# The samples' memory attention of a streaming encoder step: split float32r products against native fp32 products in 32-column tiles

## The chip, the cores and the metric

The kernel runs on one core of one Trainium2 chip. Such a core has five engines with their own instruction streams: TensorE multiplies matrices (the profile shows its products as PE and its weight loads as PEld), VectorE (DVE) and ScalarE (ACT) work on rows of data and can read TensorE's results in PSUM, GpSimd (POOL) works on SBUF, and SyncE (SP) issues most of the DMAs. The metric is the device time of one execution in microseconds (us); less is better. Data are float32 throughout. A product in plain float32 and one in "float32r" are two forms of the same TensorE instruction; the kernel reaches float32 accuracy with float32r by splitting an operand into a rounded part and the rest ("hi" and "lo"), and adding the products of the parts.

## The reference, cut to what matters

One layer of an encoder works on a prompt of 2048 frames and on 8 running streams ("samples") with 16 new frames each, 128 rows in all. After the mixer each group does cross-attention with 4 heads of 256 channels into 256 memory tokens. For the prompt the keys and values are computed; every sample brings its own cached ones (`cache_mem_k`, `cache_mem_v`, 8 x 256 x 4 x 256 each).

```python
def memory_attention(h, mk, mv, w_mq, w_mo):
    B, T, _ = h.shape
    q = (h @ w_mq).reshape(B, T, MEM_HEADS, MEM_HEAD_DIM)
    s = jnp.einsum("bthd,bmhd->bhtm", q, mk, preferred_element_type=jnp.float32) * (MEM_HEAD_DIM ** -0.5)
    p = jax.nn.softmax(s, axis=-1)
    o = jnp.einsum("bhtm,bmhd->bthd", p.astype(mv.dtype), mv).reshape(B, T, D_MODEL)
    return o @ w_mo
```

For the samples this means: each sample multiplies its 16 query rows of 4 heads with its own keys, takes a softmax over 256 tokens per head, and multiplies with its own values.

## The kernel before, in words

The kernel goes through the layer in stages: the prompt's memory keys and values, the input projection with the convolution, band attention, the output projection (`mixout`), cross-attention of the prompt (`phase_cross`) joined with the feed-forward network's first half, and its second half (`down`). The program is recorded by Python code; a scheduler with a timeline model then fixes the order of the instructions on each engine, and puts in the waits. That order is fixed before the run.

The change lies in `mixout` and in the generator `cross_sample` that it drives. `mixout` handles 17 tiles of 128 rows (the samples' tile first, then 16 of the prompt). For each it loads attention and convolution results (`prep`, line 974), splits them, multiplies them with the eight resident blocks of the output weights (`mm3h`, line 298: 48 products of 128x512 per tile, three split products for two halves of eight blocks), and normalises the result into `x1` (lines 1029 to 1035). When the samples' tile is done, `cross_sample` starts. It is a Python generator with a `yield` after each small step; `mixout` lets it take one step after every second block of weights, from the third tile on, so that its work stands between the main products.

The steps of `cross_sample`: normalise the samples' rows; transpose them (`transposed`, lines 1066 to 1078, eight 128x128 transposes, then split); multiply with `w_mq` (`dense`, line 1080); scale and transpose the queries; for each of 16 jobs (sample s, half) load one 128x1024 block of keys (line 1063), split it (`split`, line 1054: ScalarE copies the hi part at line 1057, VectorE subtracts at line 1058), and multiply; softmax; transpose the probabilities; 16 jobs with the values in the same way; transpose the result, multiply with `w_mo`, normalise into `x2`. `Ahead` keeps two jobs loaded (and split) in front of the one being multiplied. Loads go into three buffers ("wf") of 128x1024.

How one job is multiplied before the change: a sample's query block has only 16 columns. GpSimd keeps two zeroed 128x8x128 blocks (`pads`) and copies the 16 columns of the sample's hi part to its own place and those of its lo part to the place 64 columns further (`pad`, lines 1099 to 1104; `blank`, line 1095, clears them again). With that block as weights, one product gives the hi and the lo result in different rows, and the other samples' rows get zeros added. Each job then has eight products of 128x256 in float32r:

```python
for k in range(4):
    kk = 4 * half + k
    for y, r in enumerate((kh, kl)):
        nc.tensor.matmul(sc[:, kk // 2, :], cur[:, kk, :], r[:, k * NM:(k + 1) * NM], ...)
```

After four samples `gather` (line 1110) adds the two halves of the rows into `z`. The jobs with the values (line 1185) look the same. The PSUM tile "so" (4 KB per partition, one buffer) holds in turn the result of `w_mq`, the scores of four samples, the outputs of four samples, and the result of `w_mo`; tile "p" (three buffers) takes transposes.

Other lines that the profile names: L776 and L794 are products in plain float32 of the samples' band attention, L847 transposes there; L937 transposes the sums of the band attention's softmax (128x16); L982 spreads them (16x128); L1225 splits weights for the next stage; L325 to L327 transpose and split the first tiles of the next stage.

Of the kernel before, what the change touches and what calls it, by code (L numbers as in the profile page):

```python
# [140 lines left out]
class Build:  # L141
# [773 lines left out]
    def selectors(self):  # L915

        nc = self.nc
        pool = self.wp = Region().lay(self.fa, 27.5, ("eye", 0.03125, 1), ("rc", 0.03125, 2)).lay(
# [37 lines left out]
    def mixout(self, ctx):  # L956
        nc, A = self.nc, self.A
        sbF, sbR = self.sbF, self.sbR
        fr, ff = self.flex(ctx, (4096, F32R)), self.fa
        pool = (Region().lay(sbF, 34.5, ("wf", 4, 3), ("gbc", 4, 1))  # L960
                .at("ct", 2, (ff, [2, 10])).lay(ff, 0, ("an", 2, 1)).lay(ff, 5, ("po", 4, 1))
                .lay(ff, 12, ("junk", 2, 1), ("xt", 4, 2), ("sh", 4, 1), ("ss", 0.03125, 6), ("rstd", 0.03125, 6),
                     ("nmx", 0.03125, 1), ("sm", 0.03125, 1), ("ri", 0.03125, 1)).lay(ff, 28, ("sgain", 4, 1))
                .lay(fr, 0, ("pad0", 4, 1), ("pad1", 4, 1))
                .at("mh", 4, (sbR, [40, 88])).at("ml", 4, (sbR, [44, 92]))
                .lay(sbR, 96, ("sTh", 4, 1), ("sTl", 4, 1))
                .at("kvh", 4, (sbR, [64, 80]), (fr, [8])).at("kvl", 4, (sbR, [104, 84]), (fr, [12])))
# [73 lines left out]
    def cross_sample(self, pool, ps_so, ps_p):  # L1041
# [24 lines left out]
        def transposed(src, dst, scale=1.0):  # L1066
            th = self.t(pool, [P, KC, P], F32R, "sTh", 1)
            tl = self.t(pool, [P, KC, P], F32R, "sTl", 1)
            for half in range(2):
                sl = slice(4 * half, 4 * half + 4)  # L1070
                pt = self.t(ps_p, [P, 4, P], F32, "p")
                for k in range(4):
                    nc.tensor.transpose(pt[:, k, :], src(4 * half + k), self.ident[:, :])
                nc.scalar.activation(th[:, sl, :], pt[:, :, :], AF.Copy, scale=scale)
                nc.vector.scalar_tensor_tensor(tl[:, sl, :], pt[:, :, :], scale, th[:, sl, :].bitcast(F32),
                                               ALU.mult, ALU.subtract)
                yield
            dst += [th, tl]

# [8 lines left out]
        def places(s):  # L1088


            own = s * DEC_S
            other = (own + 64) % P
            return [slice(o, o + DEC_S) for o in (own, other)]

        def blank(s):
            for c in places(s):
                nc.gpsimd.memset(pads[s % 2][:, :, c].bitcast(F32), 0.0)

        def pad(s, T):
            if s >= 2:  # L1100
                blank(s - 2)
            for c, src in zip(places(s), T):
                nc.gpsimd.tensor_copy(pads[s % 2][:, :, c], src[:, :, s * DEC_S:(s + 1) * DEC_S])
            return pads[s % 2]

        def clear():
            for s in (DEC_B - 2, DEC_B - 1):
                blank(s)

        def gather(dst, src, g):  # L1110

            own, other = slice(g * 64, g * 64 + 64), slice(64 - g * 64, P - g * 64)
            nc.scalar.copy(dst[own], src[other])
            nc.vector.tensor_tensor(dst[own], dst[own], src[own], ALU.add)

        col = lambda x: lambda k: x[:, k * P:(k + 1) * P]
        flat = lambda x: x[:, :, :].rearrange("p a b -> p (a b)")

        hT = []
        yield from transposed(col(h), hT)  # L1120
# [5 lines left out]
        qT = []  # L1126
        yield from transposed(col(q), qT)

        z = self.t(pool, [P, MH, NM], F32, "sh", 1)
        jobs = [(s, b) for s in range(DEC_B) for b in range(2)]  # L1130

        def keys(s, half):
            return split(load(A["cache_mem_kT"][s, half])[:, :])

        ahead = Ahead([lambda j=j: keys(*j) for j in jobs])
        pd = pad(0, qT)
        yield
        for x, (s, half) in enumerate(jobs):
            kh, kl = next(ahead)
            cur = pd  # L1140
            if half == 1 and s + 1 < DEC_B:
                pd = pad(s + 1, qT)
            if half == 0 and s % 4 == 0:
                sc = self.t(ps_so, [P, MH, NM], F32, "so")
            for k in range(4):
                kk = 4 * half + k
                for y, r in enumerate((kh, kl)):
                    nc.tensor.matmul(sc[:, kk // 2, :], cur[:, kk, :], r[:, k * NM:(k + 1) * NM],
                                     start=s % 4 == 0 and kk % 4 == 0 and y == 0,
                                     stop=s % 4 == 3 and kk % 4 == 3 and y == 1, skip_group_check=True)  # L1150
            if half == 1 and s % 4 == 3:
                gather(z, sc, s // 4)
            yield
        clear()
        nmx = self.t(pool, [P, MH], F32, "nmx", 1)
        nc.vector.tensor_reduce(nmx[:, :], z[:, :, :], axis=AX.X, op=ALU.max, negate=True)
        sm = self.t(pool, [P, MH], F32, "sm", 1)
# [17 lines left out]
        for x, (s, b) in enumerate(jobs):  # L1175
            vh, vl = next(ahead)
            cur = pd
            if b == 1 and s + 1 < DEC_B:
                pd = pad(s + 1, pT)
# [519 lines left out]
```

## Time and profile before

| | |
|---|---|
| time, median of 3 runs | 2955.26 us (2954.59 to 2962.31) |
| profiled execution, its own time | 2962.86 us |
| its span | 2960.8 us |
| mean granted TensorE clock | 0.995 |
| TensorE products busy | 2905.3 us (98%) |
| VectorE / ScalarE / GpSimd busy | 2131.0 / 1338.0 / 1418.2 us |
| stage `mixout` with `cross_sample` | about 873 to 1150 us of the span |

A row of the profile that describes a group reads: line, engine, operation, output<-inputs by tile names, shape, count | busy time in us, mean ns of one | idle time of the engine before them and what ended it. Rows of the order of time begin with start and length in us; a count at the end merges equal neighbours, and square brackets give the idle time in front. Product records on TensorE overlap, since a product's record includes the time until its result has left the array; the pace is the distance of starts, not the length of a record. Rows by stretches give, for each engine, busy time and count, then the granted clock, the share of the DMA engines, and GB/s.

### The profile page before, as it was taken

The numbers are of one execution on the slowest core, as the hardware profiler recorded it, in microseconds if no ns is written. First come the engines' busy times: TensorE is split into PE (matmuls) and PEld (weight loads), VectorE is DVE, ScalarE is ACT, GpSimd is POOL, SyncE is SP. The second block draws the span as 40 slices with busy tenths as digits, with TensorE's granted clock in tenths as the row PEclk, the third lists the DMA queues.
The fourth block names the chain that finished last, engine by engine and source line by source line (L and its number), as shares of the span: only waits on it lengthen the run. The fifth ranks groups of instructions, "written<-read, shape, count | busy, mean of one in ns | idle before, by whom it ended". The sixth has DMA issues, their size and how long they took to land.

```text
span 2960.8 us, 45532 instructions
## 1 busy us (share of the span) xinstructions
PE 2905.3 (98%) x16680; PEld 2670.8 (90%) x16680; DVE 2131.0 (72%) x3074; ACT 1338.0 (45%) x2631; POOL 1418.2 (48%) x1334
## 2 busy tenths in 40 slices
PE   9999999989999999999999999999999999999998
PEld 8999999989987887887879999999999999888787
DVE  6787895888875666344459888787888998546666
ACT  4435465678883445233334333433344444333433
POOL 1358496731113344144457555465656775424413
PEclk9999999999999999999999999999999999999999
DMA  8735253665535656133355333544334446756664
GB/s 287 243 129 187 95 166 112 220 212 174 200 125 177 212 201 200 57 114 109 123 173 193 135 123 128 194 163 149 141 132 158 149 142 212 236 169 213 224 224 147
DMA packets 201458, 499.53 MB, mean 169 GB/s; under 512 B 19801, under 2 KB 91361, under 8 KB 192394
## 3 DMA queue, kind: packets, MB, share of 16 engines
q1 hardware_dynamic: 186306, 427.01, 43.6%
q0 software_dynamic: 14928, 69.61, 6.3%
q8 instruction: 131, 2.15, 0.3%
q14 instruction: 93, 0.76, 0.1%
HBM read 365.45 MB, written 141.81 MB: 171 GB/s over the span
## 4 chain that ended last, share of the span: by engine, by line
PE 40%; DVE 3%; DMA 3%; POOL 3%; issue 2%; ACT 1%; SPq 0%; DVEq 0%; POOLq 0%; ACTq 0%
PE psb L292 13%; PE psb L290 13%; PE psb L291 13%; DMA sbf<-in_w_down_dram 1%; PE psb L298 1%; POOL sbf L1512 1%; DMA sbf<-x 1%; DVE sbr L1582 1%; PE psb L1367 1%; DVE sbr L1390 0%; POOL sbf L348 0%; DVE sbx L1390 0%; DMA sbf<-hn 0%; DVE sbf L365 0%; DMA hn<-sbf 0%
## 5 line engine op out<-in xcount | busy, mean ns | idle before, releaser
L290 PE MATMUL psb<-sbr 128*128 128x384 f32 (+3 forms) x2808 | 941.3, 336 | 6.0 <-DVE sbx L657 2.1
L291 PE MATMUL psb<-sbr 128*128 128x384 f32 (+3 forms) x2356 | 804.4, 342 | 0.3
L292 PE MATMUL psb<-sbr 128*128 128x512 f32 (+3 forms) x1848 | 633.4, 344 | 4.6 <-DVE sbr L1582 4.4
L290 PEld LDWEIGHTS psb<-sbr 128*128 128x128 f32 x2808 | 530.3, 189 | 36.6 <-ACT sbr L1581 4.0
L292 PE MATMUL psb<-sbr,sbx 128*128 128x384 f32 (+2 forms) x1484 | 476.2, 322 | 0.0
L291 PEld LDWEIGHTS psb<-sbr 128*128 128x128 f32 x2356 | 444.9, 189 | 27.0 <-DVE sbr L340 0.9
L292 PEld LDWEIGHTS psb<-sbr 128*128 128x128 f32 x1848 | 347.9, 189 | 36.2 <-DVE sbr L1582 9.5
L298 PE MATMUL psb<-sbr 128*128 128x512 f32 x1200 | 295.0, 396 | 5.2 <-DVE flexb L1033 2.8
L1390 DVE TENSOR_TENSOR sbr<-sbf,sbr 128x512 fp32r<-128x512 f32 x258 | 264.4, 1028 | 40.5 <-ACT sbr L1389 39.6
L1389 ACT CAST sbr<-sbf 128x512 fp32r<-128x512 f32 x258 | 159.2, 620 | 278.8 <-PE psb L291 229.1
L292 PEld LDWEIGHTS psb<-sbr,sbx 128*128 128x128 f32 x1484 | 280.6, 189 | 0.1
L298 PEld LDWEIGHTS psb<-sbr 128*128 128x128 f32 x1200 | 223.6, 190 | 52.9 <-DVE flexb L1033 3.2
L523 DVE SCALAR_TENSOR_TENSOR psb<-sbf,psb 128x768 f32<-128x768 f32 (+1 forms) x290 | 264.3, 911 | 6.2
L1582 DVE TENSOR_TENSOR sbr<-sbf,sbr 128x384 fp32r<-128x384 f32 (+2 forms) x242 | 166.0, 710 | 97.5 <-ACT sbr L1581 93.8
L285 POOL TENSOR_TENSOR sbx<-sbf,sbr 128x1024 fp32r<-128x1024 f32 (+1 forms) x62 | 154.4, 2493 | 77.9 <-ACT sbr L283 63.4
L1512 POOL TENSOR_TENSOR sbf<-sbf 128x512 f32<-128x512 f32 x77 | 108.5, 1413 | 168.5 <-DMA sbf<-in_w_down_dram 166.9
L1581 ACT CAST sbr<-sbf 128x384 fp32r<-128x384 f32 (+2 forms) x242 | 112.3, 483 | 168.6 <-PE psb L291 144.1
L533 POOL TENSOR_TENSOR flexb<-flexb,flexb 128x128 f32<-128x128 f32 (+1 forms) x180 | 168.5, 936 | 26.5 <-ACT flexb L532 17.9
L290 PE MATMUL psb<-sbr,sbx 128*128 128x384 f32 (+1 forms) x524 | 170.6, 327 | 0.7 <-ACT sbr L1369 0.7
L1389 ACT CAST sbx<-sbf 128x512 fp32r<-128x512 f32 x153 | 94.7, 620 | 161.4 <-PE psb L291 150.0
L1390 DVE TENSOR_TENSOR sbx<-sbf,sbx 128x512 fp32r<-128x512 f32 x153 | 154.0, 1008 | 14.9 <-ACT sbx L1389 14.6
L1384 POOL TENSOR_TENSOR sbf<-sbf 128x512 f32<-128x512 f32 x66 | 98.3, 1489 | 108.1 <-DVE sbr L1390 50.8
(327 smaller groups left out, 6129.6 us busy)
## 6 DMA issues: line engine op xcount, KB each, us to landing
af<-flexb SPq DMA_DIRECT2D x33, 1344.0 KB, 6.2
sbf<-in_w_down_dram SPq DMA_DIRECT2D x154, 256.0 KB, 3.7
sbf<-in_w_gate_dram SPq DMA_DIRECT2D x66, 512.0 KB, 3.4
sbf<-in_w_up_dram SPq DMA_DIRECT2D x66, 512.0 KB, 3.4
sbf<-af SPq DMA_DIRECT2D x85, 384.0 KB, 4.3
sbf<-x SPq DMA_DIRECT2D x49, 512.0 KB, 3.8
sbf<-in_w_in_dram SPq DMA_DIRECT2D x48, 512.0 KB, 3.9
sbr<-ks POOLq DMA_DIRECT2D x16, 1024.0 KB, 9.1
```

The lines of the kernel that those rows point to most:

```text
L285: self.lo_engine.tensor_tensor(lo[:, c], wf[:, c], hi[:, c].bitcast(F32), ALU.subtract)
L290: nc.tensor.matmul(ps, lh, rh, start=start, stop=False, **kw)
L291: nc.tensor.matmul(ps, lh, rl, start=False, stop=False, **kw)
L292: nc.tensor.matmul(ps, ll, rh, start=False, stop=stop, **kw)
L298: nc.tensor.matmul(y[o], l, r[:, o * 512:(o + 1) * 512], start=start and x == 0, stop=stop and x == 2)
L523: nc.vector.scalar_tensor_tensor(acc if w < CW - 1 else o, src(w), cwt[:, j, w:w + 1], acc, ALU.mult, ALU.add)
L533: nc.gpsimd.tensor_tensor(o, o, v, ALU.add)
L1389: nc.scalar.copy(hs[j][:, :], src[j])
L1390: nc.vector.tensor_tensor(ls[j][:, :], src[j], hs[j][:, :].bitcast(F32), ALU.subtract)
L1512: nc.gpsimd.tensor_tensor(acc[:, :], acc[:, :], q[:, :], ALU.add if s > 0 else ALU.subtract)
L1581: nc.scalar.copy(ch[:, m], a[:, x, m])
L1582: nc.vector.tensor_tensor(cl[:, m], a[:, x, m], ch[:, m].bitcast(F32), ALU.subtract)
```

## The change

The keys and values of the samples are no longer split, and the queries no longer copied into padded blocks. A job now has four products in plain float32, one per head. Each takes 32 columns as weights (16 of the sample and 16 that only fill up: the next sample's queries, or unused rows of the probabilities) and is placed with `tile_position=(0, 32 * head)`, so that head h uses columns 32h to 32h+31 of the array and writes partitions 32h to 32h+31 of PSUM. Scores lie as (head, token) by sample. The host lays out the keys' cache so that one block holds one half of the channels of all four heads.

What follows from that: softmax runs per group of four samples, straight from PSUM (one reduction, four exponentials, a reciprocal, and four scalings, the latter on GpSimd instead of VectorE). Probabilities and outputs have sixteen 128x128 blocks to transpose instead of eight. Queries and probabilities are kept whole (`sT`), without a split. The output is copied out of PSUM after every second sample and split after its transposes, in sixteen small pieces (`token`). The `gather` steps, the blanks and the padded copies go. Splits of `w_mq` and `w_mo` stay. In SBUF some tiles move to make room for the larger `sh` and `sT`, among them the small ones of `selectors`.

```diff
-        fr, ff = self.flex(ctx, (4096, F32R)), self.fa
+        (ft, fr), ff = self.flex(ctx, (2048, F32), (2048, F32R)), self.fa
...
-        pads = [self.t(pool, [P, KC, P], F32R, f"pad{i}", 1) for i in range(2)]
-        for pd in pads:
-            nc.gpsimd.memset(pd[:, :, :].bitcast(F32), 0.0)
-            yield
+        yield
+        yield
+
+        def turn(src, k0):
+            pt = self.t(ps_p, [P, 4, P], F32, "p")
+            for k in range(4):
+                nc.tensor.transpose(pt[:, k, :], src(k0 + k), self.ident[:, :])
+            return pt
+
+        def turned(src, place):
+            th, tl = [self.t(pool, [P, KC, P], F32R, x, 1) for x in ("sTh", "sTl")]
+            for k0 in range(0, len(place), 4):
+                pt = turn(src, k0)
+                some = [p for p in place[k0:k0 + 4] if p]
+                for to, of in some:
+                    nc.scalar.copy(to(th), of(pt))
+                for to, of in some:
+                    nc.vector.tensor_tensor(to(tl), of(pt), to(th).bitcast(F32), ALU.subtract)
+                yield
+            return th, tl
...
+        def heads(out, s, x, left, right):
+            for h_ in range(MH):
+                nc.tensor.matmul(out[32 * h_:32 * h_ + 32, s % 4, :], left(h_), right[:, h_ * NM:(h_ + 1) * NM],
+                                 start=s % 2 == 0 and x == 0, stop=x == 1, tile_position=(0, 32 * h_),
+                                 skip_group_check=True)
...
-        def keys(s, half):
-            return split(load(A["cache_mem_kT"][s, half])[:, :])
...
+        qT = self.t(pool, [P, KC, P + DEC_S], F32, "sT", 1)
+        nc.gpsimd.memset(qT[:, :, P:], 0.0)
+        for k0 in range(0, KC, 4):
+            nc.scalar.copy(qT[:, k0:k0 + 4, :P], turn(col(q), k0)[:, :, :])
+            yield
+        z = self.t(pool, [P, DEC_B, NM], F32, "sh", 1)
+        nmx, sm, ri = [self.t(pool, [P, DEC_B], F32, x, 1) for x in ("nmx", "sm", "ri")]
+        ahead = Ahead([lambda s=s, x=x: load(A["cache_mem_kT"][s, x]) for s, x in jobs])
         yield
+        for s, x in jobs:
+            kx = next(ahead)
+            if x == 0 and s % 4 == 0:
+                sc = self.t(ps_so, [P, 4, NM], F32, "so")
+            heads(sc, s, x, lambda h_: qT[:, 2 * h_ + x, s * DEC_S:(s + 2) * DEC_S], kx)
             yield
+            if x == 1 and s % 4 == 3:
+                g = slice(s - 3, s + 1)
+                nc.vector.tensor_reduce(nmx[:, g], sc[:, :, :], axis=AX.X, op=ALU.max, negate=True)
+                for v in range(s - 3, s + 1):
+                    nc.scalar.activation(z[:, v, :], sc[:, v % 4, :], AF.Exp, bias=nmx[:, v:v + 1],
+                                         accum_out=sm[:, v:v + 1])
+                nc.vector.reciprocal(ri[:, g], sm[:, g])
+                for v in range(s - 3, s + 1):
+                    nc.gpsimd.tensor_scalar(z[:, v, :], z[:, v, :], ri[:, v:v + 1], None, ALU.mult)
...
+        pT = self.t(pool, [P, 2 * DEC_B, P], F32, "sT", 1)
+        for k0 in range(0, 2 * DEC_B, 4):
+            nc.scalar.copy(pT[:, k0:k0 + 4, :], turn(by_pair(z), k0)[:, :, :])
+            yield
+        of = self.t(pool, [P, DEC_B, NM], F32, "sh", 1)
+        ahead = Ahead([lambda s=s, b=b: load(A["cache_mem_v"][s, b * P:(b + 1) * P, :]) for s, b in jobs])
+        yield
+        for s, b in jobs:
+            vx = next(ahead)
+            if b == 0 and s % 4 == 0:
+                o = self.t(ps_so, [P, 4, NM], F32, "so")
+            heads(o, s, b, lambda h_: pT[:, 2 * s + b, 32 * h_:32 * h_ + 32], vx)
+            if b == 1 and s % 2 == 1:
+                nc.scalar.copy(of[:, s - 1:s + 1, :], o[:, s % 4 - 1:s % 4 + 1, :])
             yield
...
+        oT = yield from turned(by_pair(of), [token(k) for k in range(2 * DEC_B)])
...
-    o["cache_mem_kT"] = (i["cache_mem_k"].reshape(DEC_B, NM, 2, 4, P).transpose(0, 2, 4, 3, 1)
+    o["cache_mem_kT"] = (i["cache_mem_k"].reshape(DEC_B, NM, MH, 2, P).transpose(0, 3, 4, 2, 1)
                          .reshape(DEC_B, 2, P, D))
```

More of the change, by code (lines that the diff above doesn't have):

```diff
@@ L1064, in load @@
             return wf
[L1066 to L1078, printed above, removed]
         def dense(lhs, wn, y):
```

95 lines of the change are left out of this document (13 added, 82 removed).

## The prediction, made before the result was known

> **What bounds the kernel now.** I read the page first (shares of the engines), then busy time by stretches over the stage that holds the change, then the order of time on TensorE inside it.
>
> ```profile
> span 2960.8 us, 45532 instructions
> PE 2905.3 (98%) x16680; PEld 2670.8 (90%) x16680; DVE 2131.0 (72%) x3074; ACT 1338.0 (45%) x2631; POOL 1418.2 (48%) x1334
> ...
> core 0: us, PE busy (x) PEld busy (x) DVE busy (x) ACT busy (x) POOL busy (x), PEclk, DMA share, GB/s
> 873.00:940.00 67.00, 64.22 (x311) 52.63 (x310) 36.31 (x61) 28.46 (x56) 21.01 (x23) 0.97 0.48 159
> 940.00:1018.00 78.00, 78.00 (x394) 64.39 (x394) 46.92 (x57) 32.17 (x54) 29.31 (x49) 1.00 0.61 205
> 1018.00:1095.00 77.00, 77.00 (x410) 64.62 (x410) 51.27 (x62) 34.19 (x63) 34.28 (x59) 1.00 0.62 207
> 1095.00:1150.00 55.00, 50.96 (x249) 41.47 (x248) 38.12 (x31) 26.70 (x42) 26.52 (x29) 1.00 0.61 205
> ```
>
> The stage (output projection with the samples' attention between) runs from 873 to 1150 us. From 940 to 1095, where all keys and values are multiplied, TensorE has no idle time, while VectorE is busy 98 of 155 us, ScalarE 66, GpSimd 64 and the DMA engines 0.62. So inside the stage only TensorE's own time counts. Its idle time lies at two places, the start and the end:
>
> ```profile
> 910.73 1.75 PE L298 MATMUL psb<-sbr,sbx 128*128 128x512 f32 x7
> ...
> 915.59 1.65 PE L298 MATMUL psb<-sbr 128*128 128x512 f32 x3 [2.78 <-DVE flexb L1033]
> ...
> 1141.99 1.21 PE L298 MATMUL psb<-sbr,sbx 128*128 128x512 f32 x4 [0.35 <-DVE sbr L1058]
> ...
> 1145.32 1.20 PE L298 MATMUL psb<-flexb,sbx 128*128 128x512 f32 x4 [0.41 <-DVE flexb L1058]
> 1149.77 1.09 PE L325 MATMUL psb<-ident,sbf 128*128 128x128 f32 x8 [3.25 <-DVE sbr L327]
> ```
>
> The first row gives the pace of the main products: seven in 1.75 us, the last counted with its whole 0.39 us, so (1.75-0.39)/6 = 0.227 us each.
>
> **What the change takes off TensorE.** Per sample and half there were 8 products of 128x256 (four slices by two split parts), 256 in all. Their pace:
>
> ```profile
> 1056.78 0.86 PE L298 MATMUL psb<-sbr,sbx 128*128 128x512 f32 x3
> 1057.48 0.28 PE L1185 MATMUL psb<-sbr,flexb 128*128 128x256 f32 x1
> ...
> 1058.43 1.12 PE L1185 MATMUL psb<-sbr,flexb 128*128 128x256 f32 x8
> 1059.38 1.12 PE L1185 MATMUL psb<-flexb 128*128 128x256 f32 x8
> 1060.34 0.86 PE L298 MATMUL psb<-sbr 128*128 128x512 f32 x3
> ```
>
> From 1057.48 to 1060.34 stand 24 of them: 0.119 us each, 256 x 0.119 = **30.5 us** removed.
>
> **What it puts there.** 32 jobs of four native fp32 products (one per head, 32 columns of weights, 256 columns streamed). The kernel has native fp32 products elsewhere, in the samples' band attention, with 272 columns: 32 instructions in the source, 64 records, so each runs as two passes.
>
> ```profile
> L776 PE MATMUL psb<-sbf,flexb x64: 392/393/793, 632.5 to 852.4; 128*128 128x272 f32 x64
> ...
> 700.60 2.00 PE L776 MATMUL psb<-sbf,flexb 128*128 128x272 f32 x8
> ```
>
> Eight passes in 2.00 us, the last with its whole 0.392: (2.00-0.392)/7 = 0.230 us a pass, for 256 columns 0.230 x 256/272 = 0.216 us. So 128 products are 256 passes. Nothing in the trace shows two column tiles working at once, so the cost is bounded from both sides. All passes one after another: 256 x 0.216 = 55.3 us. All four heads at once: two passes per stretch of such products. In the changed program's order these 128 stand in 38 stretches (the scheduler cuts some jobs in two): 38 x 2 x 0.216 = 16.4 us. I take the middle way: products start in program order, and the order is first and second pass of head 0, then of head 1, and so on. The second pass of a head needs the same columns as its first and waits for it; the first pass of the next head uses other columns and can run beside the second pass of this one. A stretch of n products then takes 2 x 0.216 + (n-1) x (0.216 + g), where g is the start of the next head behind its weight load. g lies between 0 and the whole load of the one narrow weight block that the trace has, L937's 16 columns:
>
> ```profile
> L937 PEld LDWEIGHTS psb<-ident,sbr x16: 87/88/88, 864.0 to 1098.4; 128*16 128x16 f32 x16
> ...
> L1148 PEld LDWEIGHTS psb<-sbr,flexb x60: 186/190/192, 981.3 to 1031.7; 128*128 128x128 f32 x60
> ```
>
> L1148's loads take 0.190 us, yet its products follow at 0.119, so most of a load hides and the pace goes with its columns: 0.119 x 32/128 = 0.03. That is nearest in kind, so g = 0.03: 38 x 0.432 + 90 x 0.246 = **38.5 us** (35.9 with g = 0, 43.8 with 0.088). Net of the 30.5: +8.0 (5.4 to 13.3).
>
> Transposes go from 32 to 48 (P and the output are turned in sixteen blocks instead of eight):
>
> ```profile
> 702.67 1.03 PE L847 MATMUL psb<-ident,flexb 128*128 128x128 f32 x8
> ...
> L1073 PE MATMUL psb<-ident,flexb 128*128 128x128 f32 x32 | 4.3, 272 | 0.0
> ```
>
> Eight such in 1.03 us, (1.03-0.272)/7 = 0.108 each: 16 x 0.108 = **+1.7 us**.
>
> **Switching between whole array and tiles.** 38 stretches mean 38 round trips. The trace has two kinds of round trip among the main products:
>
> ```profile
> 1036.65 1.29 PE L298 MATMUL psb<-sbr 128*128 128x512 f32 x5
> 1037.79 0.27 PE L937 MATMUL psb<-ident,sbr 128*16 128x128 f32 x1
> 1037.81 1.40 PE L298 MATMUL psb<-sbr 128*128 128x512 f32 x5
> ...
> 1061.04 0.85 PE L298 MATMUL psb<-sbr 128*128 128x512 f32 x3
> 1061.82 0.66 PE L982 MATMUL psb<-sbr 16*128 16x128 f32 x4
> 1062.41 0.96 PE L298 MATMUL psb<-sbr 128*128 128x512 f32 x3
> ```
>
> From end to end, L937 (few columns, all rows) adds 39.21 - 37.94 - 5 x 0.227 = 0.13 us, what one 128-column pass costs anyway. L982 (few rows) adds 63.37 - 61.89 - 3 x 0.227 = 0.80 us for four products that follow each other at some 0.12: about 0.32 us too much. The new tiles have all rows and few columns, like L937: I take 0, and 38 x 0.32 = 12 us as the other end. The Trainium skill (page "TensorEngine Tiling (Array Packing)", Key Properties) says that changing the tiling mode drains TensorE; L982 agrees, L937 doesn't, and by the rule the sum below would be 12 us larger.
>
> **What is taken off or moved elsewhere.**
>
> ```profile
> L1057 ACT CAST flexb<-sbf 128x1024 fp32r<-128x1024 f32 x16 | 16.8, 1048 | 22.6 <-PE psb L1185 8.7 <-PE psb L1148 6.5 <-PE psb L298 5.7
> L1058 DVE TENSOR_TENSOR flexb<-sbf,flexb 128x1024 fp32r<-128x1024 f32 x16 | 29.6, 1853 | 18.6 <-ACT flexb L1057 18.6
> L1097 POOL MEMSET flexb<- 128x128 f32 x28 | 4.8, 201 | 38.5 <-PE psb L1148 23.4 <-PE psb L1185 15.1
> L1103 POOL CAST flexb<-sbx 128x128 fp32r<-128x128 f32 x32 | 15.1, 500 | 0.0
> L780 POOL TENSOR_SCALAR flexb<-flexb 128x272 f32<-128x272 f32 x4 | 3.8, 962 | 17.6 <-DVE flexb L779 17.6
> ...
> DMA to landing us min/median/max: 3.2/4.3/6.7
> ```
>
> 32 of 48 splits go: ScalarE -34 us, VectorE up to -59 (32 x 1.85). GpSimd loses 20 us of blanks and copies and gains eight scalings of 256 (L780's kind, 8 x 0.96 = 7.7). None of it ended a wait of TensorE between 940 and 1095, so it is worth 0 there; if that cover were gone, one split would cost 1.05 + 1.85 us once. Two new waits: a load's buffer is freed by TensorE's product instead of by the split. SyncE then holds that load, and the x and cs loads queued behind it, until job j-1 is done; the load is for job j+2, three steps of about 4.3 us (277 us over some 64 steps) later, against 4.3 to 6.7 to land: hidden, else 2 us a job at most. And the score tile in PSUM is read by the exponentials directly, so the second group of samples waits for one reduction (1.2 us) and four exponentials (0.7 each) where some 34 main products, 7.7 us, stand between: hidden.
>
> At the end of the stage the order does change. Between the samples' last output split and the first L327 stood 11 VectorE instructions, now 7; the main products over them fall from 103 to 66 (15 us). The stalls there (0.35 + 0.41 + 3.25 us) can vanish or grow by as much; seven at 1.2 to 3 us are 8 to 20. I take **-3 us**. The stall of 2.78 at 915 stands in the same order as before: 0. Fewer splits also leave less traffic beside the main products; -0.5.
>
> **The sum.** -30.5 + 38.5 + 1.7 - 3 - 0.5 = +6 us. The profiled execution took 2962.9 us (span 2960.8), so 2969 there; it was 7.6 over the median of the runs, 2955.3, on which I forecast **2961.3**, no measurable change: 0.3% (8.9 us) is what a measurement of this kernel can tell.
>
> **The rivals.**
> 1. The tiles don't overlap (slower). Passes queue one after another as L776's do at 0.230. Then 55.3 - 30.5 + 1.7 - 3.5 = +23: 2978. For it: L776 is the only evidence on fp32 passes, and none overlap there. Against: L776 uses all columns. It decides as soon as fewer than about 76 of the 90 pairs of neighbouring heads overlap: 23 - 8.9 = 14.1 us, at 0.216 - 0.03 = 0.186 saved per pair.
> 2. All four heads at once (faster). If a head's second pass waits at its own columns without holding up the next head, a stretch takes two passes and three loads' gaps: 16.4 + 90 x 0.03 = 19; 19 - 30.5 + 1.7 - 3.5 = -13: 2942. For it: the heads share neither columns nor results. Against: in the rows above products start one behind another, 0.230 apart where both need the same columns, and nothing passes a waiting one. The Trainium skill (page "TensorE: Matmul & The Clock Gate", Part 3) has column tiles start 4 ns apart, three giving 2.38 times, and also says products start in strict order; the first speaks for this rival, the second for my middle way. No run here shows either.
> 3. The switch costs what L982's does (slower): +6 + 12 = +18: 2973. Against: L937.
>
> **Chances and range.** Middle way 0.45, its own range 2953 to 2972 (g to 0.088, the end of the stage from -6 to +3). Rival 1 0.27, rival 2 0.20, rival 3 0.08. Faster: rival 2 and a sliver of the middle, 0.22. Slower by over 8.9: rivals 1 and 3 and a third of the middle, 0.35 + 0.15 = 0.50. Same: 0.28. The range takes in rivals 1 and 2 with a few us for the end of the stage: 2937 to 2982.
>
> **What would show it.** Each step: the fp32 rows of the tiles, 256 passes; a full stretch of four between main products should take 1.17 us (1.73 for rival 1, 0.5 for rival 2) from first start to the next main product; 48 transposes at 0.108; no gap beyond 0.03 at a switch (0.32 for rival 3); GpSimd's blanks gone. Wrong would be: idle TensorE between 940 and 1095 behind a key or value load or behind the exponentials, or a stall at the end of the stage longer than 4 us.

## The result, and the profile after

| | before | after |
|---|---|---|
| time, median of the runs made side by side (five each) | 2962.31 us (2954.59 to 2962.72) | 2971.79 us (2968.29 to 2975.01) |
| ratio | | 1.0041 (95% interval 1.0029 to 1.0054) |
| span of the profiled execution | 2960.8 us | 2973.1 us |

The changed kernel is slower by 0.41%, which is 12 us; the ratio is estimated from all runs and need not be that of the medians, which differ by 9.5 us. The two profiled executions differ by 12.3 us. Run again later, it gave 1.0035 (1.0023 to 1.0048). The time lies inside the predicted range, and the sign is the one that had the largest chance; but the forecast itself said "no change", and the reasons come out differently from all four stories told before.

The page of the changed kernel, its first two rows:

```profile
span 2973.1 us, 45433 instructions
...
PE 2911.9 (98%) x16696; PEld 2651.7 (89%) x16696; DVE 2070.3 (70%) x3046; ACT 1310.1 (44%) x2623; POOL 1394.4 (47%) x1281
```

VectorE has lost 61 us of work, ScalarE 28 and GpSimd 24, and the span is 12 us longer. Where that comes from is told by stretches (PE, PEld, VectorE, ScalarE, GpSimd busy; then the granted clock). First the changed kernel:

```profile
873.00:940.00 67.00, 64.22 (x311) 52.67 (x311) 36.38 (x60) 27.97 (x57) 19.27 (x21) 0.97 0.48 157
940.00:1018.00 78.00, 78.00 (x400) 56.22 (x399) 28.59 (x47) 19.57 (x49) 26.27 (x32) 1.00 0.60 199
1018.00:1095.00 77.00, 77.00 (x419) 52.57 (x419) 25.46 (x38) 18.78 (x49) 25.48 (x30) 1.00 0.59 200
1095.00:1150.00 55.00, 49.15 (x237) 35.33 (x236) 25.52 (x35) 22.50 (x50) 20.33 (x24) 0.97 0.67 229
1150.00:1235.00 85.00, 76.47 (x334) 61.52 (x333) 37.97 (x45) 31.38 (x54) 17.83 (x18) 0.94 0.39 124
```

The kernel before, in the one stretch that the prediction didn't show (the start of the next stage, cross-attention of the prompt):

```profile
1150.00:1235.00 85.00, 82.67 (x383) 68.04 (x382) 41.37 (x49) 31.22 (x59) 18.65 (x19) 0.98 0.37 120
```

From 940 to 1095, where the tiles work, TensorE is busy throughout as it was before, while VectorE's share falls from 98 to 54 us. The difference begins at 1095. From there to 1235 TensorE idled 5.85 + 8.53 = 14.4 us, before 4.04 + 2.33 = 6.4 us: 8.0 more. The granted clock was 0.97 and 0.94 against 1.00 and 0.98: lost are 0.03 x 55 + 0.06 x 85 = 6.7 us against 0.02 x 85 = 1.7, so 5.0 more. Together 13.0 us, which is the whole loss.

The same can be counted in work done. The main products of line 298 between 873 and 1250, before:

```profile
873.00:1250.00 377.00, 315.59 (x1306) 0.99 0.52 173
```

and after:

```profile
873.00:1250.00 377.00, 312.74 (x1248) 0.98 0.52 171
```

58 fewer at 0.227 us are 13.2 us. Counting them from the start of the stage shows when the changed kernel falls behind (the distance in time between the n-th main products, from the raw records of the two traces):

```
main products                      before    after
0 to 168    (start of the stage)    55.42    55.54
168 to 700  (keys and values)      155.49   153.46
700 to 870  (output transposes)     48.96    50.53
870 to 1250 (w_mo, next stage)     104.08   117.74
sum                                363.95   377.27
```

While the tiles work the changed kernel is 2.0 us ahead. Eight more transposes and late values take 1.6 back. All the rest, 13.7 us, is lost in the handover to the next stage.

The tiles themselves, in the order of time on TensorE (start, length, line, shapes, count):

```profile
998.62 1.53 PE L298 MATMUL psb<-sbr,sbx 128*128 128x512 f32 x6
1000.08 0.64 PE L1092 MATMUL psb<-sbf,flexb 128*32 128x256 f32 x8
1000.65 1.66 PE L298 MATMUL psb<-sbr 128*128 128x512 f32 x6
```

and as a group (shortest, median and longest ns; first and last start), with the transposes:

```profile
L1092 PEld LDWEIGHTS psb<-sbf,flexb x256: 106/109/110, 974.3 to 1116.6; 128*32 128x32 f32 x128
L1092 PE MATMUL psb<-sbf,flexb x256: 379/379/403, 974.3 to 1116.9; 128*32 128x256 f32 x128
...
L1054 PE MATMUL psb<-ident,flexb x48: 270/272/328, 928.7 to 1126.6; 128*128 128x128 f32 x48
```

Eight passes fill 0.64 us, of which the last pass takes 0.379: it starts 0.26 us after the first, where one behind another would take 7 x 0.216 = 1.5. So all four heads run at once. From end to end the stretch costs (1000.65 + 1.66) - (998.62 + 1.53) - 6 x 0.227 = 0.80 us: 0.216 for each of two passes, and about 0.36 that are no work.

Where these 0.36 us lie is told by the weight loads of the same stretch:

```profile
1000.08 0.16 PEld L1092 LDWEIGHTS psb<-sbf,flexb 128*32 128x32 f32 x8 [0.35 <-issue]
1000.65 0.76 PEld L298 LDWEIGHTS psb<-sbr 128*128 128x128 f32 x4 [0.41 <-ACT sbx L989]
```

Among main products a weight load starts 0.227 us ahead of its product (1000.992 and 1001.219). At the two ends of the stretch the first load and its product start together (1000.081 and 1000.083; 1000.650 and 1000.652, raw records). The first tile product comes 0.319 us after the last main product instead of 0.227, the second passes come 0.240 us after the first instead of 0.216, the next main product 0.113 us later than a third round of passes would have, and the one behind it after 0.337 instead of 0.227: 0.09 + 0.02 + 0.11 + 0.11 = 0.34 us. What makes the loads start late isn't shown.

Where TensorE stood still at the handover (idle time and its releaser in brackets):

```profile
1141.45 1.20 PE L298 MATMUL psb<-flexb,sbx 128*128 128x512 f32 x4 [3.70 <-DVE flexb L1073]
1149.28 1.73 PE L298 MATMUL psb<-sbr,sbx 128*128 128x512 f32 x4 [2.15 <-DVE sbr L1073]
1158.36 0.73 PE L298 MATMUL psb<-sbr 128*128 128x512 f32 x2 [2.20 <-ACT sbr L1188]
1160.20 15.57 PE L298 MATMUL psb<-sbr 128*128 128x512 f32 x61 [1.10 <-DVE flexb L347]
1184.26 1.46 PE L298 MATMUL psb<-sbr 128*128 128x512 f32 x4 [1.10 <-ACT sbr L1224]
1187.25 1.97 PE L325 MATMUL psb<-ident,sbf 128*128 128x128 f32 x8 [1.54 <-DVE sbr L1225]
1224.76 1.20 PE L298 MATMUL psb<-sbr 128*128 128x512 f32 x4 [1.29 <-ACT sbr L326]
1227.22 1.09 PE L1221 MATMUL psb<-ident,sbf 128*128 128x128 f32 x8 [1.26 <-DVE sbr L327]
```

In the changed kernel L1073 is the split of a block of `w_mo`. The first two rows are its product waiting for blocks, with no main product left to stand between. And each of the longer stalls has a second price, the clock (busy time by stretches, granted clock behind it):

```profile
1137.80:1141.40 3.60, 0.00 (x0) 1.00 0.31 125
1141.40:1142.90 1.50, 1.45 (x6) 0.99 0.26 96
1142.90:1146.30 3.40, 3.40 (x9) 0.50 0.66 247
1147.20:1149.20 2.00, 0.00 (x0) 1.00 0.45 176
1149.70:1153.10 3.40, 3.40 (x13) 0.50 0.75 181
```

Behind stalls of 3.70 and 2.15 us come 3.4 us at half speed each, worth 1.7 us, the first after another 1.5 us at full speed. The changed kernel has four such stretches between 1140 and 1235 (from 1142.9, 1149.7, 1159.9 and 1187.2), the kernel before one (from 1150.9). The Trainium skill (page "TensorE: Matmul & The Clock Gate", Part 1) describes a gate with two states, full and half, that goes by a window of about 3.4 us; the length and the two values agree with these rows.

The traces say more on the price of a stall. In each of the 13 the starts of the half-speed stretches lie whole multiples of 3.413 us apart (here two, three and eight). Taken in slots of that grid from 900 to 1300 us, 37 slots at full speed were followed by half speed: 36 held 1.91 us or more of idle TensorE, one held 1.54 (the kernel before with four empty steps). The 1450 that stayed at full speed held 1.83 us or less. So what counts here is the idle time that falls into one slot: 1.99 of the 3.70 us fell into the slot that ends at 1142.9, and stalls of 1.10 and 1.54 us together put 1.96 into the one that ends at 1187.2.

Why is the split of `w_mo` late? The chain on VectorE (start, length, line; idle and releaser in brackets):

```profile
1134.07 1.23 DVE L1189 TENSOR_TENSOR sbr<-sbf,sbr 128x1024 fp32r<-128x1024 f32 x1 [2.78 <-ACT sbr L1188]
1138.85 1.41 DVE L1032 SCALAR_TENSOR_TENSOR flexb<-psb,flexb,sbf 128x512 f32<-128x512 f32 x2 [3.55 <-DMA x<-flexb]
1140.18 1.22 DVE L1073 TENSOR_TENSOR flexb<-sbf,flexb 128x1024 fp32r<-128x1024 f32 x1
1141.31 3.42 DVE L1073 TENSOR_TENSOR sbx<-sbf,sbr 128x1024 fp32r<-128x1024 f32 x1
1144.66 3.43 DVE L322 SCALAR_TENSOR_TENSOR sbf<-sbf 128x1024 f32<-128x1024 f32 x1
```

L1032 normalises the last tile of the output projection. It waits 3.6 us until the store of the tile before has read the only buffer "po", and the splits of `w_mo` stand in the queue behind it. A second wait of that time (us in total, times, longest):

```profile
ACT sbr L1072 <- DMA sbf<-in_w_mo_dram: 6.8, 2, 3.6
```

ScalarE's half of the split waits for blocks of `w_mo` that are still on their way, and `w_mo` is loaded through the same three buffers as the values, which are in use until later here. The step count accounts for that. `mixout` gives the generator one step per two blocks of weights, that is per 12 products of line 298, and the change turned two transposing passes of two steps into two of four. The output's transposes before:

```profile
1119.51 1.03 PE L1073 MATMUL psb<-ident,flexb 128*128 128x128 f32 x8
```

and after, the first and the last of four groups:

```profile
1119.36 0.60 PE L1054 MATMUL psb<-ident,flexb 128*128 128x128 f32 x4
...
1126.22 0.60 PE L1054 MATMUL psb<-ident,flexb 128*128 128x128 f32 x4
```

The first begins when it did before, although the changed kernel was 2 us ahead until then; the last ends 6.3 us later (1126.82 against 1120.54). By count the last stands behind 840 of the 864 products that come ahead of those with `w_mo` (17 tiles and `w_mq`, 48 each), before behind 813. So 24 of them are left, 5.4 us, to cover what follows, where 51 were, 11.6 us.

### The profile page after: what moved, and what is told of

It reads as the page before. It is cut to its first block, busy times and chain, and to the rows that moved or that the text cites. A ratio compares the mean times of both kernels' runs of the same rounds, so it can differ in the third digit from the quotient of the medians.

```text
span 2973.1 us, 45433 instructions
## 1 busy us (share of the span) xinstructions
PE 2911.9 (98%) x16696; PEld 2651.7 (89%) x16696; DVE 2070.3 (70%) x3046; ACT 1310.1 (44%) x2623; POOL 1394.4 (47%) x1281
## 3 DMA queue, kind: packets, MB, share of 16 engines
q8 instruction: 131, 2.15, 0.3%
## 4 chain that ended last, share of the span: by engine, by line
PE 41%; DMA 3%; DVE 3%; POOL 2%; issue 1%; ACT 0%; DVEq 0%; POOLq 0%; SPq 0%; ACTq 0%
PE psb L292 13%; PE psb L291 13%; PE psb L290 13%; DMA sbf<-in_w_down_dram 1%; PE psb L298 1%; POOL sbf L1476 1%; DMA sbf<-x 1%; PE psb L1331 1%; DMA sbf<-hn 1%; DVE sbr L1546 0%; POOL sbf L348 0%; DVE sbr L1354 0%; DVE sbx L1354 0%; DMA hn<-sbf 0%; DVE flexb L1416 0%
```

## The experiments

Two theories to start with. Theory 1: the loss is one of pace; four steps more move the product with `w_mo` out from under the main products. Theory 2: the new work itself, or the next stage's own splits, cost at the handover whatever the pace. Each time is a median; the ratio is to the kernel before, run beside it on the same chip (2964.27 us for rows two to five, 2960.61 for the first row and rows six to eight, 2964.67 for the last three).

| run | median us | ratio to before (95%) |
|---|---|---|
| changed kernel again | 2971.95 | 1.0035 (1.0023 to 1.0048) |
| changed, paced | 2968.95 | 1.0017 (1.0008 to 1.0026) |
| before, four empty steps | 2965.67 | 1.0007 (0.9998 to 1.0017) |
| paced, halves merged | 2961.00 | 0.9986 (0.9977 to 0.9994) |
| paced, whole array (one run) | 2996.85 | |
| paced, rate 1.15 | 2959.44 | 0.9994 (0.9984 to 1.0004) |
| before, rate 1.15 | 2965.40 | 1.0009 (1.0000 to 1.0017) |
| paced, merged, rate 1.15 | 2954.55 | 0.9978 (0.9969 to 0.9988) |
| changed, rate 1.15 | 2961.59 | 0.9990 (0.9978 to 1.0003) |
| changed, a buffer more for the last tile | 2971.32 | 1.0024 (1.0013 to 1.0035) |
| paced, merged, rate 1.20 | 2974.83 | 1.0039 (1.0025 to 1.0053) |

**The changed kernel with the old number of steps.** Two groups of transposes per step in the probabilities and in the output.

```diff
-                yield
+                if len(place) == KC or k0 % 8:
+                    yield
...
-            yield
+            if k0 % 8:
+                yield
```

> The changed kernel with two groups of transposes per step instead of one for the probabilities and for the output, so that the generator has 64 steps as before the change and not 68; everything else as changed. Theory 1 (the four added steps push the product with w_mo, its loads and splits behind the last main products, and the 11 us are lost at the end of the stage): 0 +- 4 us against the kernel before, the idle time of TensorE between 1130 and 1165 us falls from about 9 us to the 5 of before. Theory 2 (the new small pieces and the store that VectorE waits for cost it, whenever they come): +8 to +12 as the changed kernel.

Measured: 1.0017, so some 7 of the 12 us are back and 5 stay. Neither expectation was met in full. The trace shows what stays: TensorE waits for the splits of `w_mo` only 0.41 and 0.74 us, but behind them the next stage's own split is waited for, and a stall of another place has grown from 1.54 to 1.78 us:

```profile
1151.35 1.97 PE L325 MATMUL psb<-ident,sbf 128*128 128x128 f32 x8 [4.39 <-DVE sbr L327]
...
1182.72 1.09 PE L325 MATMUL psb<-ident,sbf 128*128 128x128 f32 x8 [1.78 <-DVE sbr L1227]
1218.65 1.20 PE L298 MATMUL psb<-sbr 128*128 128x512 f32 x4 [1.29 <-ACT sbr L326]
```

**The kernel before with four empty steps**, in the same two places.

```diff
-        def transposed(src, dst, scale=1.0):
+        def transposed(src, dst, scale=1.0, more=0):
...
-                yield
+                for _ in range(1 + more):
+                    yield
```

> The kernel before with one empty step behind each of the two halves of the transposes of the probabilities and of the output: 68 steps, no work added. Theory 1: +8 to +12 us, with the product with w_mo and its loads some 12 us later and TensorE idle behind its splits. Theory 2: 0 +- 4 us.

Measured: 1.0007, some 2 us, where theory 1 had said 8 to 12 and theory 2 up to 4. Its last two stretches:

```profile
1095.00:1150.00 55.00, 51.01 (x258) 41.96 (x257) 36.50 (x30) 29.02 (x42) 24.26 (x32) 1.00 0.67 230
1150.00:1235.00 85.00, 80.41 (x362) 65.39 (x362) 39.11 (x49) 30.93 (x60) 16.93 (x17) 0.96 0.35 112
```

Idle 8.6 us and 3.4 lost to the clock: 12.0, against 8.1 in the kernel before and 21.1 in the changed one. VectorE's normalisation of the last tile didn't wait for a store here. Its output transposes stand where the changed kernel's last ones do, behind 840 products. So late steps have no fixed price; it depends on what they run into. Theory 1 in its simple form falls.

**Both halves of a sample multiplied together** (on the paced kernel), so that there are 25 stretches of tile products instead of 37, with the same products.

```diff
-        for s, x in jobs:
-            kx = next(ahead)
+        for s in range(DEC_B):
+            ks = [next(ahead)]
+            yield
+            ks.append(next(ahead))
...
-            heads(sc, s, x, lambda h_: qT[:, 2 * h_ + x, s * DEC_S:(s + 2) * DEC_S], kx)
+            for x in range(2):
+                heads(sc, s, x, lambda h_: qT[:, 2 * h_ + x, s * DEC_S:(s + 2) * DEC_S], ks[x])
```

The values likewise; loads run one job ahead instead of two.

> As a1_pace, but both halves of a sample are multiplied together (loads one ahead instead of two): 25 stretches of tile products among the main products instead of 37. If a round trip into the column tiles and back costs 0.35 us as the trace of the changed kernel reads, -4 us against a1_pace. If that time is the tiles' own work and not the switch, 0 +- 2. If the shorter lead of the loads shows, TensorE idles in front of the tile products and it is above a1_pace.

Measured: 2961.0 against 2968.95, 8 us less. A merged stretch in its order of time:

```profile
999.62 1.07 PE L1093 MATMUL psb<-sbf,flexb 128*32 128x256 f32 x16
1000.63 3.01 PE L298 MATMUL psb<-sbr 128*128 128x512 f32 x12
```

Sixteen passes hold up the next main product for 1.01 us from the first start; eight did for 1000.65 - 1000.08 = 0.57. The second job adds 0.44, two passes, and no second switch. From the 168th to the 870th main product, between which both kernels do all tile products and the same transposes without idle time, this kernel needs 197.91 us, the paced one 203.33: 5.42 less. Fewer jobs are cut in two, so by the raw records there are 70 rounds (passes that run at once) instead of 76: 6 x 0.216 = 1.3 us. The other 4.1 us over 12 stretches are 0.34 each, which confirms the price of a switch. Of the rest, 2.4 us lie in a handover that fell out better (870th to 1250th: 109.02 against 111.46), which was not expected.

**The same passes on the whole array**, 128 columns of weights and no tiles; the heads are computed on top of each other, so the result is not the attention's. Not shown in the diff: `left` hands over 128 columns, and `start` and `stop` are set once per job.

```diff
-                nc.tensor.matmul(out[32 * h_:32 * h_ + 32, s % 4, :], left(h_), ..., tile_position=(0, 32 * h_))
+                nc.tensor.matmul(out[:, s % 4, :], left(h_), ...)
```

> As a1_pace, but the four native fp32 products of a job take 128 weight columns each and the whole array, without a tile position (so they compute the four heads on top of each other, and the attention's result is not the reference's). Eight passes of 0.216 us a job, one after another, no switch: 55 us for 32 jobs against the 29 us that the tiles took in the changed kernel, so +22 to +28 us against a1_pace if the four tiles really work at once. If the records of the tiles are only stamped together and their work is serial, 0 +- 4.

Measured, in one run: 28 us more than the paced kernel. Its order of time:

```profile
1000.10 3.10 PE L298 MATMUL psb<-sbr,sbx 128*128 128x512 f32 x12
1003.05 1.89 PE L1093 MATMUL psb<-sbf,flexb 128*128 128x256 f32 x8
1004.58 1.72 PE L298 MATMUL psb<-sbr 128*128 128x512 f32 x6
```

From end to end 6.30 - 3.20 - 6 x 0.227 = 1.74 us, which is 8 x 0.216: no overlap and no switch. 32 x 1.74 = 55.7. From the 168th to the 870th main product this kernel needs 231.19 us against the paced kernel's 203.33, 27.9 more, which is the whole difference. So the tiles' 37 stretches cost 55.7 - 27.9 = 27.8: 76 rounds x 0.216 = 16.4 of work, and 11.4 at the switches (0.31 each on average, since eight stand beside other small products). So the tiles do work at once, four heads for the price of one. That saves 39 us, of which the switches give 11 back.

**A faster pace.** The rate of steps per two blocks goes from 1.0 to 1.15, in the paced kernel, in the kernel before, and in the paced and merged kernel; the changed kernel as it was ran beside them.

```diff
-RATE = 1.0
+RATE = 1.15
```

> As a1_pace (the changed kernel in 64 steps), with the steps let out 1.15 times as fast (RATE 1.15), so that the output's transposes stand after 728 of the stage's 912 main products and not after 810, and the product with w_mo has main products over it. Theory 1 (what is lost at the end of the stage is the product with w_mo without cover): -4 to -8 us against a1_pace, that is 0 to -3 against the kernel before, with less than 3 us of idle TensorE between the last output transpose and the next stage's second transposes. Theory 2 (the stall there comes from the next stage's own splits and norms on VectorE): as a1_pace, +3 to +7 against the kernel before.

> The kernel before with RATE 1.15 and nothing else. Theory 1: -3 to -6 us against the kernel before, because the product with w_mo gets cover there too; against a4_rate115 then only the products themselves count, 30.6 us of split products against 29 us of tiles and 1.7 us of transposes: 0 +- 2. Theory 2: 0 +- 3 against the kernel before.

> As a4_rate115 with both halves of a sample multiplied together (27 stretches of tile products against 33). By 0.35 us a round trip -2 us against a4_rate115 and, with theory 1, -3 to -7 against the kernel before; by theory 2 as a2_merged_pace, -4 +- 2. If the loads' shorter lead counts at this pace, TensorE idles in front of tile products.

> The changed kernel once more, beside the others on one chip, for the differences to it: +9 to +15 us against the kernel before, with the idle time and the half-clock stretches between 1130 and 1230 us again. If its first profile's stalls were of that execution alone, the trace will show fewer and the time stays the same.

Measured: the paced kernel at 1.15 is level with the kernel before (0.9994), the kernel before at 1.15 gains nothing (1.0009, where 3 to 6 us of gain were expected), and the merged one is faster than both kernels of this case: 0.9978, 6 us below the one before, and some 5 us below the paced one at this rate, where 2 were expected. The changed kernel repeated its loss, with the same stalls (3.73, 2.22, 2.20, 1.08, 1.10, 1.53, 1.29, 1.25 us) and half-speed stretches at the same four places. At 1.15 the changed arithmetic is thus some 4 to 6 us below the old one at the same rate (0.9994 against 1.0009; 2959.44 against 2965.40 us), and 9 to 11 below with merged halves. What all three keep is a pair of stalls at the next stage's own transposes and splits, 6 to 8 us together, with 10.2 us at half speed behind the first; less than 3 us of idle time, as theory 1 had it there, did not come.

**The faster pace alone**, on the changed kernel with its four-step transposes. The last of the output's stands behind 768 products then.

> The changed kernel as it is, its sixteen-block transposes in four steps each, with steps taken 1.15 times as often: output transposes end after 768 of 912 main products instead of 840. Theory 1 (only the bare end of the stage costs): as the paced kernel at the same rate, 2958 to 2963, so 9 to 14 below the changed kernel. Theory 2 (the four steps more, the small pieces of the output's split, or the tiles themselves cost in the covered part too): 2966 or more.

Measured: 0.9990 (0.9978 to 1.0003), level with the kernel before; the time that theory 1 gave. By stretches:

```profile
1095.00:1150.00 55.00, 50.57 (x232) 40.82 (x231) 32.97 (x42) 26.34 (x57) 27.66 (x29) 0.95 0.61 210
1150.00:1235.00 85.00, 82.72 (x381) 68.48 (x380) 41.71 (x48) 30.12 (x58) 15.00 (x17) 0.97 0.33 106
```

Idle 6.7 us, 5.3 lost to the clock: 12.0 instead of 21.1. One number in the source takes the whole loss away, with the same transposes, the same small pieces of the split and the same tiles. So none of these costs the 12 us wherever it stands; the loss hangs on where the steps fall. The rate moves all steps, though, and the kernel before with its last transposes at the same late place lost 2 us only: the late place of `w_mo` costs 12 us together with what this kernel meets there, not alone.

**The wait on the store alone.** The last tile's normalised result goes into a tile of its own. The order of instructions is that of the changed kernel on every engine; only this wait goes.

```diff
-                .lay(sbR, 96, ("sTh", 4, 1), ("sTl", 4, 1)).lay(ft, 0, ("sT", 8, 1))
+                .lay(sbR, 96, ("sTh", 4, 1), ("sTl", 4, 1)).lay(ft, 0, ("sT", 8, 1)).at("pz", 4, (ft, [4]))
...
-            po = self.t(pool, [P, D], F32, "po")
+            po = self.t(pool, [P, D], F32, "po" if i < len(order) - 1 else "pz")
```

> The changed kernel with one tile more: the normalised result of the last of the 17 tiles of the output projection goes into a tile of its own, so its normalisation (L1032) needn't wait until the store of the tile before has read the shared one. The order of all instructions on every engine is that of the changed kernel. In the changed kernel VectorE waits 3.6 us there with splits of w_mo queued behind it. Theory 1 (the loss lies in the chain VectorE, split of w_mo, product, which stands bare at the end of the stage): the wait is gone, TensorE's 3.70 us stall at 1141 falls to under 1 us, a half-clock stretch of 3.4 us goes with it, and the time falls from 2972 to 2965 to 2969. Theory 2 (the next link, ScalarE's wait for the block of w_mo or GpSimd's work, is as late): the stalls only move, 2970 to 2973.

Measured: 1.0024 (1.0013 to 1.0035), against 1.0041 and 1.0035 for the changed kernel: 3 to 5 us less by the midpoints, but the intervals overlap, so the time alone doesn't show a gain. In the profiled executions the distance from the 870th to the 1250th main product fell from 117.74 to 112.58 us. The stalls became:

```profile
1142.88 1.19 PE L298 MATMUL psb<-sbr 128*128 128x512 f32 x4 [1.84 <-ACT sbr L326]
...
1148.36 1.21 PE L298 MATMUL psb<-flexb,sbx 128*128 128x512 f32 x4 [0.21 <-DVE flexb L1073]
1154.79 0.73 PE L298 MATMUL psb<-sbr 128*128 128x512 f32 x2 [3.84 <-ACT sbr L1188]
1156.27 15.69 PE L298 MATMUL psb<-sbr 128*128 128x512 f32 x61 [0.75 <-DVE flexb L347]
```

The 3.70 and 2.15 behind L1073 are gone but for 0.21, and with them two of the half-speed stretches; but a block of the next stage's weights (L1188), which had waited 2.20, now waits 3.84. In the stretches from 1095 to 1235 TensorE's idle time falls only from 14.4 to 12.3 us, and the granted clock loses 3.4 us instead of 6.8. Both theories were partly right: the wait was on the path, and of the 5.6 us of stall that went with it some 3.5 came back at other links.

**A rate of 1.20** for the paced and merged kernel.

> The paced kernel with both halves of a sample multiplied together, at a rate of 1.20 instead of 1.15: 30 stretches of tile products instead of 27, so some 1 us more for switches by the theory that a switch there and back costs 0.35 us; the end of the stage is covered in both. Expected 2953 to 2958, as at 1.15. By the theory that earlier steps still shorten the handover, 2950 or less.

Measured: 1.0039, by the ratios 18 us more than at 1.15, where 1 us was expected. A miss by either theory. The stall on TensorE:

```profile
1140.56 8.19 PE L298 MATMUL psb<-sbr 128*128 128x512 f32 x24 [6.61 <-DVE flexb L1032]
```

and what VectorE waited for there:

```profile
1139.75 1.41 DVE L1032 SCALAR_TENSOR_TENSOR flexb<-psb,flexb,sbf 128x512 f32<-128x512 f32 x2 [4.43 <-DMA x<-flexb]
```

It is the store of the tile before once more: the scheduler placed the same normalisation so that it meets the buffer still in use, and this time TensorE itself waits, for the PSUM tile that L1032 reads. The pace that was good at 1.15 isn't a rule; each order of the handover has its own waits.

## Why the prediction was right or wrong

**Right.** The split products cost what their rows said, and so did the transposes: four in 0.60 us give (0.60 - 0.272) / 3 = 0.109, as predicted 0.108. TensorE had no idle time between 940 and 1095, neither behind the loads, whose buffers now come free later, nor behind the exponentials; the 61 us less on VectorE, 28 on ScalarE and 24 on GpSimd were worth nothing there.

**Mis-sized: the tile products, +38.5 us.** The middle way said that a head's second pass holds up the next head. It doesn't. The raw records have the first passes of the four heads 7 ns apart, then the four second passes, each 0.24 us after its head's first. A full stretch holds up the next main product for 0.57 us, where 1.17 was named for the middle way, 1.73 for rival 1 and 0.5 for rival 2. So rival 2's mechanism was the true one, without the 0.03 per weight load: 38 x 0.432 = 16.4 us. The page "TensorE: Matmul & The Clock Gate" of the Trainium skill, Part 3, has tiles start some 4 ns apart; the trace has 7, for two-pass products. Its other rule, products in strict order, was read too hard in the prediction: it holds for the starts of the four products, but one of two passes doesn't block the next head in between.

**Mis-sized: the switch, 0.** The prediction took L937 as the nearest row. The nearest was L982: a stretch between main products costs 0.36 us by the end-to-end count above, 0.34 by the merged kernel's 4.1 us for 12 stretches. 38 x 0.36 = 13.7 us. Rival 3, given 0.08, was right in its mechanism. The Trainium skill (page "TensorEngine Tiling (Array Packing)", Key Properties) has the drain at a change of mode; these runs show a price of 0.34 to 0.36 us at such a change, which agrees, though not that a drain makes it. That a single product with 16 columns shows none of it remains unexplained.

The two errors nearly cancel, which is luck: 16.4 + 13.7 = 30.1 us of tiles against 30.5 removed, where the prediction had 38.5. With the transposes that makes +1.3. Measured up to the 870th main product are -0.3, some 1.5 us less. The raw records place it: seven of the 38 stretches stand right behind the four products of 16x128 (L981 there, L982 before). A stretch alone delays the main products by 0.78 us and L981 alone by 0.79, but both together by 1.36, so that each of the seven saves some 0.2 us.

**The step that failed: the end of the stage, -3 us.** It came out at +13. The prediction counted VectorE's instructions between the last split of the samples' output and the next stage (fewer) and saw the cover shrink from 103 to 66 main products, and then let the first outweigh the second. What it left out is when the chain of `w_mo` begins, and the diff shows that: `turned` has one `yield` per four blocks, sixteen blocks make four steps, and each step is worth 12 main products. The prediction followed how the order changed there, but not that the whole tail moved. The rate alone, which moves it back under the main products, took the loss away; lateness alone, in the kernel before, cost 2 us. It also priced a stall at its own length; at this place 5 of the 13 us are the half-speed clock that follows. Its own sign for this step, a stall longer than 4 us, did not show: the longest was 3.70, and the loss came in several shorter ones.

**The base.** The forecast stood on a median of 2955.3; beside the changed kernel the same kernel gave 2962.3. Of the 10.5 us between 2961.3 and 2971.8 this is 7. In ratios the forecast was 1.002, the result 1.0041.

**Open.** Why four late steps cost 12 us with the tiles and 2 with the split products. The wait on the store may be 3 to 5 of the difference: the run without it points that way, with intervals that overlap. The rest seems to lie in how the scheduler orders the first 200 products of the next stage (two stalls of 1.29 and 1.26 us at 1225 exist in the changed and in the paced kernel and in none of the kernels at rate 1.15); no run changed that order alone.

## What to carry to other kernels

Tiles of columns multiplied four small products for the price of one here, but each switch between tiles and the whole array cost some 0.35 us: count stretches, not products, and let neighbouring jobs share one. Work that a generator lays under a main loop has a tail: a few more steps move it out from under the loop, so count the steps that a rewrite adds and read what covers the tail. What that costs hangs on what it meets, 12 us in one kernel here and 2 in the other. A stall can cost 1.7 us more through the clock, by how much of it falls into one slot of 3.41 us, and most of the idle time that the freed wait gave up came back at others, so the experiment, not the first wait in the trace, tells the gain.

## What the runs showed of the hardware that was not expected

Products in plain float32 on four column tiles interleave pass by pass: first passes 7 ns apart, second passes 0.24 us later, 0.64 us for eight passes that take 1.89 us on the whole array. A weight load of 32 columns took 0.109 us; inside a stretch the loads of the second passes ran beside the first passes, but at a switch the first load started with its product and not ahead of it. Half speed followed where about 1.9 us or more of idle time fell into one slot of a fixed grid of 3.41 us. And a VectorE subtraction of 128x1024, 1.2 us mostly, took 3.4 us at the handover (1141.31 above), so a late split there is later than its row elsewhere says. GpSimd's elementwise product of 128x1024 (L1033) ran from 1140.34 to 1143.65 beside it, and the split ended 1.08 us after that; VectorE's next instruction, of 3.43 us, ended 1.09 us after GpSimd's L1189 did. In the kernel before two splits of 3.40 and 3.41 us end 1.09 and 1.08 us after a GpSimd instruction of that size (L1034). That looks like waiting for the other's end, but no run took GpSimd's work away.
